# Copying a shifted matrix in 4 KB pieces down a column, 128 rows per DMA, in place of half rows of 16 KB, 1024 rows per DMA

## Chip, cores, metric

One core of a Trainium2 chip; the seven other cores are idle. The metric is the device time of one execution in microseconds. The kernel before takes 812.68 us (median of 3 runs, 810.87 to 816.9). On the chips of the experiments the same kernel takes 814 to 827 us, so every comparison in time is with runs of the kernel before on the same chip.

## The reference

```python
x = np.random.randn(8192, 8192).astype(np.float32)   # 268 MB

def reference(x):
    return np.fft.ifftshift(x)     # both halves swapped, in both directions
```

Every element moves by 4096 rows and 4096 columns, modulo 8192. No arithmetic is done. The longest run of bytes that stays together is half a row: 4096 x 4 bytes = 16 KB.

## The kernel before

Four quadrants, each copied from memory to memory by four DMAs, all issued from one queue:

```python
    quads = [
        ((0, hr), (0, hc), (hr, R), (hc, C)),
        # ... the other three quadrants in the same way (cut)
    ]
    nsplit = 4
    for (or0, or1), (oc0, oc1), (ir0, ir1), (ic0, ic1) in quads:
        step = (or1 - or0) // nsplit                 # 1024 rows
        for s in range(nsplit):
            a = s * step
            b = a + step
            nc.sync.dma_start(
                out=out[or0 + a : or0 + b, oc0:oc1],
                in_=x[ir0 + a : ir0 + b, ic0:ic1],
            )
```

Of the kernel before, what the change touches and what calls it, by code (L numbers as in the profile page):

```python
# [1 line left out]

# [4 lines left out]


@with_exitstack  # L10
def kernel(
    ctx: ExitStack,
    tc: tile.TileContext,
    x: bass.AP,
    out: bass.AP,
):
    nc = tc.nc

    R, C = x.shape
    hr = R // 2  # L20
    hc = C // 2

    quads = [
        ((0, hr), (0, hc), (hr, R), (hc, C)),
        ((0, hr), (hc, C), (hr, R), (0, hc)),
        ((hr, R), (0, hc), (0, hr), (hc, C)),
        ((hr, R), (hc, C), (0, hr), (0, hc)),
    ]

    engines = [nc.sync]  # L30
    nsplit = 4
    k = 0
    for (or0, or1), (oc0, oc1), (ir0, ir1), (ic0, ic1) in quads:
        rows = or1 - or0
        step = rows // nsplit
        for s in range(nsplit):
            a = s * step
            b = a + step
            eng = engines[k % len(engines)]
            k += 1  # L40
            eng.dma_start(
                out=out[or0 + a : or0 + b, oc0:oc1],
                in_=x[ir0 + a : ir0 + b, ic0:ic1],
            )


# [1 line left out]
_INS = ['x']  # L48
_OUTS = [((8192, 8192), 'float32')]


def kernel(**inputs):
    import numpy as _np
    import concourse.bacc as _bacc
    import concourse.tile as _tile
    from concourse import mybir as _mybir
    from concourse.bass_utils import run_bass_kernel_spmd as _run

    nc = _bacc.Bacc("TRN2", target_bir_lowering=False, num_devices=1)  # L59
    arrays, args = {}, []  # L60
    for name in _INS:
        a = _np.ascontiguousarray(inputs[name])
        if a.dtype.kind in "iu":
            a = a.astype(_np.int64)
        arrays[f"in_{name}_dram"] = a
        args.append(nc.dram_tensor(f"in_{name}_dram", a.shape, _mybir.dt.from_np(a.dtype), kind="ExternalInput").ap())
    for i, (shape, dtype) in enumerate(_OUTS):
        dt = _mybir.dt.from_np(_np.dtype(dtype))
        args.append(nc.dram_tensor(f"out_{i}_dram", shape, dt, kind="ExternalOutput").ap())
    with _tile.TileContext(nc) as tc:  # L70
        kernel(tc, *args)
    r = _run(nc, [arrays], core_ids=[0])
    got = tuple(r.results[0][f"out_{i}_dram"] for i in range(len(_OUTS)))
    return got[0]
```

## Time and profile before

| | before |
|---|---|
| median | 812.68 us |
| profiled span | 811.5 us |
| DMAs, each | 16, 16.8 MB |
| data packets, each | 16384, 16 KB |
| busy time of the 16 DMA engines | 99.3% |
| memory read + written | 662 GB/s |

The lines behind this table are in the prediction. The compute engines have nothing to do, so only the DMA part of the page speaks. "Busy" there means that an engine had a packet under way; whether the packet moved at full speed shows only in how long it took. A data packet here is one unbroken piece that one engine moves; a completion write is a packet of 4 bytes with which an engine reports that its share of a DMA is done. The time that a data packet takes beyond the commonest, shortest one of its size is called its stall.

### The profile page before, as it was taken

Reading aid. Unit: us, or ns where it says so; the run is one execution under the profiler, and the core shown is the slowest. Engines: PE = TensorE matmul, PEld = TensorE weight load, DVE = VectorE, ACT = ScalarE, POOL = GpSimd, SP = SyncE. Lnnn points to the kernel's source line nnn. Section 1 sums busy time; section 2 is a strip of 40 time slices with the busy share of each in tenths; the row PEclk is TensorE's granted clock in tenths of the full one; section 3 lists DMA queues with packets and bytes.
Section 4 is the critical chain, followed back from the end, with each engine's and each line's share of the span. In section 5 each row is a group of like instructions: output and inputs, shape, how many; then the busy total and the mean of one; then the engine's idle time right before and its main releaser. Section 6 shows DMA issues by size and latency. Waiting matters only on the chain. (4 is left out here: it accounts for less than half of the span.)

```text
span 811.5 us, 61 instructions
## 1 busy us (share of the span) xinstructions
POOL 0.2 (0%) x4
## 2 busy tenths in 40 slices
POOL 0000000000000000000000000000000000000000
DMA  9999999999999999999999999999999999999998
GB/s 298 328 328 333 312 337 332 326 334 329 332 334 329 329 329 334 331 331 334 338 340 333 332 334 339 334 333 337 338 333 337 334 333 338 332 334 341 328 339 287
DMA packets 16640, 268.44 MB, mean 331 GB/s; under 512 B 256, under 2 KB 256, under 8 KB 256
## 3 DMA queue, kind: packets, MB, share of 16 engines
q1 hardware_dynamic: 16640, 268.44, 99.3%
HBM read 268.44 MB, written 268.44 MB: 662 GB/s over the span
## 5 line engine op out<-in xcount | busy, mean ns | idle before, releaser
L59 POOL MEMSET const-bfloat16-1.0<- 128x1 bf16 x1 | 0.1, 102 | 0.0
L59 POOL MEMSET const-uint8-127<- 128x1 uint8 x1 | 0.1, 101 | 0.0
L59 POOL MEMSET const-float32-0.0<- 128x1 f32 x1 | 0.1, 99 | 0.2 <-issue 0.2
L59 POOL MEMSET const-float32-1.0<- 128x1 f32 x1 | 0.1, 98 | 0.0
## 6 DMA issues: line engine op xcount, KB each, us to landing
out_dram<-in_x_dram SPq DMA_DIRECT2D x16, 16384.0 KB, 158.0
```

Of the source, the lines that this page charges most:

```text
L59: nc = _bacc.Bacc("TRN2", target_bir_lowering=False, num_devices=1)
```

## The change

The intent is to give the memory a better order of addresses. Half rows are cut in four pieces of 4 KB; one DMA takes one column of pieces, 128 rows deep, so that an engine's next piece lies one row (32 KB) further on, and not right behind the last.

```diff
+ROWS_PER_DMA = 128
+PIECE = 1024
...
-    for (or0, or1), (oc0, oc1), (ir0, ir1), (ic0, ic1) in quads:
-        rows = or1 - or0
-        step = rows // nsplit
-        for s in range(nsplit):
             ... (cut)
-            eng.dma_start(
-                out=out[or0 + a : or0 + b, oc0:oc1],
-                in_=x[ir0 + a : ir0 + b, ic0:ic1],
+    for row in range(0, R, ROWS_PER_DMA):
+        src = (row + hr) % R
+        for col in range(0, C, PIECE):
+            oc = (col + hc) % C
+            nc.sync.dma_start(
+                out=out[row : row + ROWS_PER_DMA, col : col + PIECE],
+                in_=x[src : src + ROWS_PER_DMA, oc : oc + PIECE],
             )
```

More of the change, by code (lines that the diff above doesn't have):

```diff
@@ L21 @@
     hc = C // 2
-    quads = [
-        ((0, hr), (0, hc), (hr, R), (hc, C)),
-        ((0, hr), (hc, C), (hr, R), (0, hc)),
-        ((hr, R), (0, hc), (0, hr), (hc, C)),
-        ((hr, R), (hc, C), (0, hr), (0, hc)),
-    ]
-    engines = [nc.sync]
-    nsplit = 4
-    k = 0
-    for (or0, or1), (oc0, oc1), (ir0, ir1), (ic0, ic1) in quads:
-        rows = or1 - or0
-        step = rows // nsplit
-        for s in range(nsplit):
-            a = s * step
-            b = a + step
-            eng = engines[k % len(engines)]
-            k += 1
-            eng.dma_start(
-                out=out[or0 + a : or0 + b, oc0:oc1],
-                in_=x[ir0 + a : ir0 + b, ic0:ic1],
+    for row in range(0, R, ROWS_PER_DMA):
[5 more added lines that the diff above has]
+                in_=x[src : src + ROWS_PER_DMA, oc : oc + PIECE],
             )
```

## The prediction

> **What bounds the kernel now.** I read the page from the top, then its queue lines, then the issues, then the packets one by one. The kernel is pure copying, memory to memory, with no compute: part 1 has four memory fills on POOL, 0.2 us in all, and the chain of part 4 ends with them, so neither says anything about the end. The slices and the queue lines do:
>
> ```profile
> DMA  9999999999999999999999999999999999999998
> GB/s 298 328 328 333 312 337 332 326 334 329 332 334 329 329 329 334 331 331 334 338 340 333 332 334 339 334 333 337 338 333 337 334 333 338 332 334 341 328 339 287
> DMA packets 16640, 268.44 MB, mean 331 GB/s; under 512 B 256, under 2 KB 256, under 8 KB 256
> ...
> q1 hardware_dynamic: 16640, 268.44, 99.3%
> HBM read 268.44 MB, written 268.44 MB: 662 GB/s over the span
> ```
>
> All 16 DMA engines are occupied all the time (99.3%), at a level rate of 326 to 341 GB/s in most slices; there is no head or tail to win (the first slice has 298, the last 287). Of the 16640 packets, 256 are the completion writes (16 DMAs by 16 engines) and 16384 the data: 268.44 MB / 16384 = 16 KB, one half row each.
>
> Occupied is not the same as running at full speed. From the trace's packet records: the mean data packet lasts 787 ns, the median 731, and 1024 of them per engine make 1024 x 0.787 = 806 us of the 811.5. But the shortest last 608 ns, and 35% are within 7 ns of that; the tail reaches 2.05 us. 608 ns for 16 KB is 26.9 GB/s, an engine's own pace. Had all run so, an engine would need 1024 x 0.608 = 623 us. So 183 us of each engine's time is packets waiting on memory. That is the quantity the change can touch.
>
> The issue side is not the limit:
>
> ```profile
> L41 SPq DMA_DIRECT2D out_dram<-in_x_dram x16: 582/49353/95664, 0.7 to 652.6; - x16
> ...
> DMA to landing us min/median/max: 53.7/158.0/199.5
> ```
>
> An issue into an empty queue took 0.58 us; the median of 49 us is SP held back by a full queue (one 16.8 MB DMA takes 16.8 / 0.331 = 50.7 us). The last issue is in place long before the end. The completion records also show that the 16 engines finish each DMA within 1.0 to 2.7 us of each other, even after 800 us. They advance together, within about three of their packets.
>
> **What the Trainium skill says.** "HBM Reference", Specifications (TRN2), gives 716 GB/s for the memory that a pair of cores shares. The trace has 662 GB/s of reads and writes together, 92% of that, if x and out both lie in that one memory. I take this as the ceiling: 536.87 MB / 716 = 750 us, as an estimate from that page, plus the 5 us at the ends.
>
> "DMA: Bandwidth & Descriptors", Latency and other measured facts, row "HBM row pitch at large powers of two": copies of 128 rows of 16 KiB ran at 207 GB/s per direction with a pitch of 512 KiB, 164 at 2 MiB, 103 at 4 and 8 MiB; 4 KiB of padding restored the rate, 192 B did not. It calls the mechanism (streams in lock step that fall on the same memory channels) an inference. It bears directly on this case: engines here advance together. No view says which rows an engine gets. If each gets a consecutive run, which is how I read the change's own words, then engine e starts 64 rows x 32 KB = 2 MiB after engine e-1. The broad mixture of full-speed and stalled packets agrees with streams that collide now and then; it does not prove it.
>
> "DMA: Bandwidth & Descriptors", Why small descriptors are slow, gives about 3 cycles per packet as fixed overhead. At its 850 MHz that is 3.5 ns, times 3072 more packets per engine = 11 us on the 623 us of full-speed time (estimate). Of the same page, the section on its rules recommends at least 1 MiB per DMA; here the DMAs shrink to 0.5 MiB. The trace before shows only 16 MiB DMAs, so it neither agrees nor disagrees.
>
> **The change, part by part.**
>
> Bytes: unchanged, 268.44 MB each way.
>
> DMAs: 16 become 8192/128 x 8192/1024 = 64 x 8 = 512, each 128 rows x 4 KB = 524 KB, so 8 data packets per engine. At today's 331 GB/s one such DMA is 1.58 us of work. SP needs about 0.58 us to issue one (the shortest of the row above; I have no issue of the new shape), plus some tens of ns between issues: 512 x 0.65 = 333 us, beside the transfers. The issuer is thus needed about 40% of the time. The trace has eight completion semaphores in turn, so up to eight DMAs, 8 x 1.58 = 12.7 us of work, should be in flight; the first packet starts 1.4 us after the first issue, so the latency of a DMA (estimate 1.4 + 1.6 + 1 = 4 us) fits inside. Cost on the path: 0, with some risk.
>
> Completion writes: 16 x 16 = 256 become 8192. Each lasts 9 ns in the packet records, and the number of active engines doesn't dip around them (16.0 to 16.1 of 16 before and after). So 512 x 9 ns = 4.6 us per engine in place of 0.14: +4.5 us.
>
> Data packets: 1024 of 16 KB per engine become 4096 of 4 KB. At full pace that is about 152 ns each, plus the overhead: 623 + 11 = 634 us. That isn't the bound while memory allows at most 750, so 0 on the path; it eats some slack.
>
> Memory side, where the sum is decided: the distance between two engines working at the same time falls from 2 MiB to 8 rows x 32 KB = 256 KiB, below the pitch at which the skill still has the full rate. An engine's requests in flight[...] now lie in several rows and not in one or two long runs, so a busy place in memory holds up a smaller part of them. Against it, all engines work in one 4 KB column at a time, on reads and on writes; only the row bits of the address tell them apart. If 60% of the gap to the ceiling is recovered: the stream goes from 806 to 806 - 0.6 x (806 - 750) = 772 us. With +4.5 for completion writes and 5.5 for the ends as now: about 782 us, 3.8% faster.
>
> **The rivals.**
>
> 1. The shared memory is simply full. At 92% of the nominal rate with reads and writes mixed, there may be nothing to recover, whatever the order. For it: the level GB/s row, and engines that keep together as under fair sharing. Against it: 35% of the packets run at the engine's own pace, which is odd for a resource that is always full. Then the time is 806 + 4.5 + 5.5 = 816 us, the same.
>
> 2. 4 KB pieces are worse for memory. Four visits to a row in place of one long run, and the 32 KB stride keeps the low address bits equal over all 16 engines and over source and destination (they differ by 16 KB in column). If those bits choose the channel, collisions grow. For it: the skill's row shows that regular pitches can halve the rate. Against it: there the pitches up to 512 KiB were harmless. A 5 to 15% loss would make 850 to 930 us.
>
> 3. The small DMAs bind: SP's issue, or the waits for a semaphore to come round, take over. It would need over 1.58 us per issue, 2.7 times what the shortest one took. If it came to 1.7 us, 512 x 1.7 = 870 us. I hold this least likely.
>
> 4. The ceiling isn't one memory's 716 GB/s (x and out may lie apart), and the new order removes nearly all stalls. Then the engines bind: 634 + 4.5 + 5.5 = 644 us. Unlikely, as I'd expect both tensors in the core's own memory.
>
> **Range and chances.** I give the recovery (main case) 0.52, rival 1 a good 0.24, rivals 2 and 3 together 0.24. The recovery centres at 770 to 785, bounded by 760 or so where the ceiling is reached; rival 4 lies under the range, and the heavier half of rival 2 above it. That leaves 745 to 855 for eight in ten.
>
> **What would show it right or wrong.** Right: DMA share still 99% or so, GB/s at 340 to 350 in every slice, packets of 4 KB with a mean of 185 to 192 ns (787 / 4 = 197 now) and a larger share near 152 ns, completion writes still about 9 ns, SP's issues mostly held back by a full queue. Rival 1: a mean packet of 197 ns and 331 GB/s. Rival 2: DMA share of 99% with packets clearly over 200 ns. Rival 3: DMA share that drops to 90% or less, with gaps between packets and SP's issues back to back. The working is wrong in its basis if the full-pace packet isn't near 152 ns, or if an engine isn't given consecutive rows.

## The result, and the profile after

The changed kernel takes 824.36 us (median of 4 runs, 820.41 to 825.46) against 813.75 us for the kernel before in 4 runs. The ratio is 1.0114, 95% interval 1.0076 to 1.0152: clear of 1. (Ratios here are the mean time of one kernel's fast runs over that of the other's in the same rounds, so not quite the ratio of the medians.) So the change cost 1.1%, where 3.8% had been forecast as gain.

The slices, queue and issue lines of the changed kernel's page, and the line of its issues (ns each, shortest, median and longest) from the view of the tile:

```profile
DMA  9999999999999999999999999999999999999998
GB/s 298 325 330 328 330 329 329 330 333 331 329 327 331 326 326 333 328 329 331 327 330 331 329 330 328 327 331 329 331 330 328 337 326 333 331 333 328 331 335 289
DMA packets 73733, 268.50 MB, mean 328 GB/s; under 512 B 8193, under 2 KB 8193, under 8 KB 73729
...
q1 hardware_dynamic: 73728, 268.47, 99.3%
...
HBM read 268.44 MB, written 268.44 MB: 656 GB/s over the span
...
out_dram<-in_x_dram SPq DMA_DIRECT2D x512, 512.0 KB, 12.7
...
L33 SPq DMA_DIRECT2D out_dram<-in_x_dram x512: 511/511/737, 0.7 to 806.0; - x171
```

The 8193 packets under 512 B are the completion writes (512 DMAs by 16 engines) and one instruction fetch; the other 65536 are the pieces. Engines are busy for 99.3% of the span as before, and most slices, 31 of 40, are a little lower than before. The engines have no gap; the issuer is held back by its own completions, as its waits show (engine, line, what it waited for, us in total, times, longest):

```profile
SPq L33 <- DMA out_dram<-in_x_dram: 534.4, 503, 2.0
```

534 us of SP's 819 are waiting, and an issue takes 0.511 us in the median. It has eight DMAs out at a time (12.7 us from issue to landing, 8 x 1.59 = 12.7).

The difference between the two kernels is in the packet records of the two traces:

| packets of the profiled run | before | after |
|---|---|---|
| data packets per engine, bytes | 1024 of 16 KB | 4096 of 4 KB |
| commonest time of one (full pace) | 611 ns | 159 ns |
| share of packets within 7 ns of that time | 35% | 85% |
| mean | 786.8 ns | 197.3 ns |
| 99th percentile | 1412 ns | 769 ns |
| all data packets, per engine | 805.6 us | 808.2 us |
| completion writes, 9 ns each, per engine | 0.14 us | 4.62 us |

Two things look right and are traps. Of the packets 85% now run at full pace, which looks like the hoped-for order; but the rest are stalled the longer, and the mean of four pieces is 4 x 197.3 = 789 ns, against 787. At full pace alone an engine would now need 4096 x 159 ns = 651 us, where it needed 1024 x 611 ns = 626; its stalls came down from 180 us to 157, and the total stayed. The engines became slower by themselves, and waited less by nearly as much. And the sum seems to close perfectly: 2.6 us more for data and 4.5 us more for completion writes are the 7.1 us by which the span grew (811.5 to 818.6). Since the engines are never idle in either kernel, the packet times *must* add up to the span; the sum says nothing about what caused the growth. The experiments below show that the completion writes did not.

### The profile page after: what moved, and what is told of

It is laid out like the page before. It is cut to its first block, busy times and chain, and to the rows that moved or that the text cites. A ratio compares the mean times of both kernels' runs of the same rounds, so it can differ in the third digit from the quotient of the medians.

```text
span 818.6 us, 557 instructions
## 1 busy us (share of the span) xinstructions
POOL 0.2 (0%) x4
## 2 busy tenths in 40 slices
DMA packets 73733, 268.50 MB, mean 328 GB/s; under 512 B 8193, under 2 KB 8193, under 8 KB 73729
## 3 DMA queue, kind: packets, MB, share of 16 engines
q1 hardware_dynamic: 73728, 268.47, 99.3%
## 6 DMA issues: line engine op xcount, KB each, us to landing
out_dram<-in_x_dram SPq DMA_DIRECT2D x512, 512.0 KB, 12.7
```

## The experiments

Theory F, formed from the result: the 16 engines together are held by what the memory takes in reads and writes, some 660 GB/s, whatever the order. Rival C: collisions of address streams stall the packets, so that order and distance matter. Rival P: the size of the piece itself costs. Rival R: each packet meets a stall of its own, whatever else runs. (The diffs below are shortened: where they name ROWS_PER_DMA and PIECE, the kernels that ran have the numbers written out.)

### Piece and DMA size apart

**p4k_1024rows**, the pieces of the change with the DMA depth of before:

```diff
-ROWS_PER_DMA = 128
+ROWS_PER_DMA = 1024
```

> 4 KB pieces down a column as in the changed kernel, but 1024 rows per DMA as in the kernel before: 64 DMAs, 1024 completion writes. Theory F (the memory that x and out share is full with some 660 GB/s of reads and writes, whatever the order; the 1.1% lost by the change is the completion writes, 512 x 9 ns = 4.6 us per engine, and about 2.5 us from the pieces): 1.003 of the kernel before, the mean data packet 197 ns. Rival P (the pieces cost it all): 1.01. Rival C (what stalls the packets is where the addresses fall, and engines 2 MiB apart collide more than engines 256 KiB apart): mean data packet clearly off 197 ns, over 205, and 1.04 or more.

Measured: 841.62 us, ratio 1.0188 (1.0138 to 1.0237). Its completion writes take 0.62 us per engine, and still it loses, so the completion writes are not where the loss is. Its mean packet was 202.0 ns; the changed kernel itself, run again on a later chip (below), had 201.6. The mark that rival C had set, 205, was not reached; the ratio is above F's 1.003 and also above rival P's 1.01. Part of it is an uneven end: in the slices of its page (the GB/s row, 40 equal slices of 21 us) the last one has 209.

```profile
GB/s 291 325 325 322 322 321 327 325 321 322 320 324 321 319 330 319 322 321 315 328 321 327 329 317 329 322 324 324 319 328 323 310 333 326 323 326 319 330 322 209
```

**p16k_32rows**, the other way round: 16 KB pieces, as many DMAs and completion writes as in the changed kernel:

```diff
-ROWS_PER_DMA = 128
-PIECE = 1024
+ROWS_PER_DMA = 32
+PIECE = 4096
```

> 16 KB pieces as in the kernel before, but 32 rows per DMA: 512 DMAs of 0.5 MB, 8192 completion writes as in the changed kernel. Theory F: the completion writes alone, +4.5 us, so 1.005 to 1.006 of the kernel before, mean data packet still 787 ns. Rival P: 1.000. Rival C: engines now 64 KiB apart and not 2 MiB, so the mean data packet moves away from 787 ns by 3% or more.

Measured: 825.13 us, ratio 0.9986 (0.9939 to 1.0032), mean packet 794 ns. Its records hold 4.61 us of completion writes per engine, and the time has not grown. So the prediction's "+4.5 us" is not in the time (a ratio of 1.0054 lies outside the interval). That an engine which is stalled for a quarter of its time does its 9 ns writes at nobody's cost is a reading of this, not measured by itself. The 794 ns are to be taken beside 787 with care: the kernel before was profiled on the first chip alone, and takes 1.6% longer on this one. Nor did engines 64 KiB apart, in place of 2 MiB, gain anything.

### Fewer engines

Row counts that 16 does not divide leave some engines without work. The loop is the same in all of these; it copies 16 KB pieces:

```diff
+    for row in range(0, R, hr):
+        src = (row + hr) % R
+        for col in (0, hc):
+            oc = (col + hc) % C
+            a = 0
+            for n in COUNTS:    # k8: 4 x 1016, 4 x 8;  k12: 4 x 996, 108, 4
+                                # k13: 4 x 1014, 39, 1;  k14: 4 x 1022, 8
+                nc.sync.dma_start(
+                    out=out[row + a : row + a + n, col : col + hc],
+                    in_=x[src + a : src + a + n, oc : oc + hc],
+                )
+                a += n
```

**k8**

> 16 KB pieces, row counts of 1016 and 8 that let only 8 of the 16 DMA engines work. Theory F: 8 engines at their own pace ask the memory for 8 x 26.9 x 2 = 431 GB/s, far below 660, so the stalls vanish: mean data packet 608 to 620 ns, 2048 x 0.61 = 1250 us. Rival C (collisions of streams): the stalls fall about with the number of streams, mean packet 690 ns, 1420 us. Rival R (a stall that each packet meets by itself, as from latency or refresh): 787 ns, 1615 us.

**k12**

> The same with 12 of 16 engines (row counts 996, 108 and 4). Theory F: the 12 ask for 646 GB/s at their own pace, just below the limit, so the time is 1365 x 0.608 = 830 us plus a little queueing, 835 to 860 us, although a quarter of the engines is idle. Rival C: mean packet 735 ns or so, 1005 us. Rival R: 1075 us.

Measured: k8 takes 1249.55 us with a mean packet of 611.2 ns; k12 takes 839.48 us with 612.9 ns. Slices, packets and traffic of k12's page:

```profile
DMA  6777777777777777777777777777777777777776
GB/s 280 326 315 319 325 317 323 323 325 322 325 322 325 322 325 322 325 323 322 320 325 323 325 323 325 323 325 323 325 323 325 323 325 323 325 319 321 324 324 260
DMA packets 16640, 268.44 MB, mean 320 GB/s; under 512 B 256, under 2 KB 256, under 8 KB 256
...
q1 hardware_dynamic: 16640, 268.44, 74.9%
HBM read 268.44 MB, written 268.44 MB: 641 GB/s over the span
```

As theory F had said (1250 us, and 835 to 860), the stalls are gone in both. In k12 the engines are busy 75% of the time, that is, a quarter of them stands idle at any time, and the kernel is 1.5% slower than with all 16. This is the central result. Twelve engines meet practically no stall while they draw 641 GB/s; four more engines add 1.5% in speed and, in the kernel before, 787 - 608 = 179 ns of stall to each packet. Rival R (787 ns) is out, and so is C in the form that was put down (690 and 735 ns). One more thing changed beside the number of engines: with these row counts an engine's share is 127 or 83 rows, so that engines, if each gets consecutive rows, no longer lie a power of two apart, as they do in every run with all 16. The next two runs answer that.

**k13** and **k14** (shares of 78 and 73 rows) ask how the step from 12 to 16 runs, and whether fewer streams could do better than 16.

> 13 of 16 engines, 16 KB pieces (row counts 1014, 39, 1). Run with 12 engines hardly a packet stalled at 641 GB/s. Theory F1 (a fixed ceiling of 650 to 660 GB/s on this chip): 13 engines could do 1260 x 0.608 = 766 us by themselves, the memory holds them to about 820 us, ratio 0.99 to 1.00, mean packet 640 to 650 ns. Theory F2 (the ceiling is higher, and too many streams at once bring it down): 770 to 795 us, ratio 0.94 to 0.97, mean packet 612 to 630 ns.

> 14 of 16 engines (row counts 1022 and 8). F1: the time of 16 engines, ratio 0.99 to 1.00, mean packet 690 to 700 ns. F2: 750 to 800 us, ratio 0.92 to 0.97, mean packet 640 to 680 ns.

Measured: k13 846.73 us, ratio 1.0278 (1.025 to 1.0305); k14 870.0 us, ratio 1.0564 (1.0539 to 1.0589). Both expectations fell: more engines than 12 made it *slower*, until with 16 it is fast again. The mean packets of 16 KB, 648.9 and 690.4 ns, are just what F1 had said. While all their engines work, the packet records show what one more engine does (stretch from 5 to 45 us of each trace; k12 and p16k_32rows ran on one chip, k13 and k14 on another):

| engines | run | each way | mean packet |
|---|---|---|---|
| 12 | k12 | 324 GB/s | 611 ns |
| 13 | k13 | 322 GB/s | 659 ns |
| 14 | k14 | 326 GB/s | 704 ns |
| 16 | p16k_32rows | 326 GB/s | 800 ns |

The rate stays, and each packet takes longer in proportion to the number of engines. The stalls come back at distances of 78 and 73 rows, so it was not the odd distance that removed them in k12: it was the smaller demand.

The time of k13 and k14 goes elsewhere. Slices of k14:

```profile
DMA  7888888888887888858888887687888868878754
GB/s 289 328 331 326 329 331 323 325 325 334 326 319 306 328 332 324 327 244 313 323 319 322 325 325 296 272 320 299 323 323 319 331 252 328 326 310 324 276 217 176
```

The rate starts at the same 326 to 331 GB/s as with 16 engines, then has dips, and ends at 217 and 176. The completion records say why: of the first DMA's 14 engines, with 73 packets each, six finished 45.9 to 46.8 us after its first packet had started, and eight after 55.8 to 56.6 us; at full pace it would be 44.6. In k13, with 78 packets each (47.7 us at full pace), five finished after 48.9 to 49.3 us and eight after 53.5 to 54.0. So there are two groups of engines, 8 and the rest, and the limit seems to be shared out to groups, not engines: 331 GB/s in halves is 165 each; six engines want 6 x 26.9 = 161 and get 155, while eight want 215 and get 170, or 21 each. In k13 five want 135 and get 130, and the eight have 190. Since the rows are dealt out evenly, the larger group ends last, alone: the last slice but one of k14, with 217 GB/s, is at the 215 that eight engines reach by themselves in k8. This reading is from completion times and rates; the records don't name the engines.

### One direction at a time

**load_only** and **store_only** give wrong results on purpose:

```diff
+    pool = ctx.enter_context(tc.tile_pool(name="t", bufs=8))   # load_only
+    for row in range(0, R, 128):
+        for col in (0, hc):
+            t = pool.tile([128, hc], mybir.dt.float32)
+            nc.sync.dma_start(out=t, in_=x[row : row + 128, col : col + hc])
+    nc.sync.dma_start(out=out[0:128, 0:hc], in_=t)
```

In store_only one tile of zeros goes to all of `out` in the same loop.

> Wrong result on purpose: x is only loaded, in 128 DMAs of 128 rows of 16 KB, to eight on-chip buffers in turn; one tile is stored at the end. If it is the sum of reads and writes that is full, not the reading: all engines at their own pace, mean packet 608 to 620 ns, 630 to 645 us. If reading alone were the limit at 331 GB/s: 810 us.

> Wrong result on purpose: one on-chip tile of zeros stored 128 times over the whole of out. If the sum is full: mean packet 608 to 620 ns, 630 to 645 us. If writing alone were the limit at 331 GB/s: 810 us.

Measured: 639.36 and 638.1 us, mean packets 615 and 617 ns. A few lines of each page, load first:

```profile
DMA packets 18577, 270.55 MB, mean 424 GB/s; under 512 B 2064, under 2 KB 2064, under 8 KB 2064
...
HBM read 268.44 MB, written 2.10 MB: 424 GB/s over the span
```

```profile
DMA packets 18433, 268.45 MB, mean 422 GB/s; under 512 B 2048, under 2 KB 2048, under 8 KB 2048
...
HBM read 0.00 MB, written 268.44 MB: 422 GB/s over the span
```

Neither reading nor writing alone is held at 331 GB/s; all 16 engines run at their own pace when each byte touches the memory once.

### Order and distance of the pieces

Four kernels on one chip. **after_again** is the changed kernel unaltered.

> The changed kernel once more, unaltered, as the yardstick on this chip for the three beside it: 1.011 of the kernel before, as on record (1.008 to 1.015).

Measured: 834.64 us, ratio 1.013 (1.0112 to 1.0148), mean packet 201.6 ns.

**p4k_same_row** takes two pieces of each of 64 rows in one DMA:

```diff
+    for row in range(0, R, 64):
...
+            for b in (0, 1):
+                nc.sync.dma_start(
+                    out=out[row : row + 64, col : col + hc].rearrange("r (a b f) -> r b a f", a=2, b=2)[:, b],
+                    in_=x[src : src + 64, oc : oc + hc].rearrange("r (a b f) -> r b a f", a=2, b=2)[:, b],
+                )
```

> 4 KB pieces and 512 DMAs as in the changed kernel, but each DMA takes two pieces, 8 KB apart, of each of 64 rows, so every other step of an engine stays in its row. If the order of the pieces matters as the change intends (one row apart is better): slower than the changed kernel by 2% or more. If only the size of the piece matters (theory F, ceiling a little lower for 4 KB): 1.01, within 0.5% of the changed kernel.

Measured: 844.44 us, ratio 1.0248 (1.0215 to 1.0282), 1.2% slower than after_again. That lies between the two expectations. The slices of the two kernels, after_again first:

```profile
GB/s 290 322 320 328 322 327 319 325 326 325 323 325 319 327 324 325 329 322 328 319 326 326 324 329 326 325 328 320 325 324 327 320 324 327 321 321 326 326 320 276
```

```profile
GB/s 241 293 295 304 314 328 332 317 327 327 327 321 324 327 324 328 328 318 321 313 324 331 319 323 330 325 319 324 321 329 333 319 330 319 320 326 327 323 326 269
```

After the first five slices the rates are alike, around 324. The loss is in the start: 49 + 29 + 25 + 24 + 8 = 135 GB/s short over slices of 21 us, or 135 x 21 / 324 = 9 us, nearly the whole difference (844.44 - 834.64 = 9.8). So this other way of cutting is worse than going down the column, the change's idea, but in the one profile only in the first 100 us. Why this order starts slowly is not known.

**p2k_256rows** halves the piece and **p16k_4096rows** spreads the engines furthest:

```diff
-ROWS_PER_DMA = 128
-PIECE = 1024
+ROWS_PER_DMA = 256      # p16k_4096rows: 4096
+PIECE = 512             # p16k_4096rows: 4096
```

> 2 KB pieces down a column, 256 rows per DMA, so still 512 DMAs of 0.5 MB and 8192 completion writes; twice the packets. If the piece is what lowers the ceiling: 1.02 or more of the kernel before, more than the changed kernel. If not: as the changed kernel, 1.01. The engines alone would need 8192 x 83 ns = 680 us (152 ns / 2 plus the 7 ns that a packet costs at 4 KB), so they don't bind.

> 16 KB pieces, 4096 rows per DMA, so 4 DMAs, and engines that work 256 rows = 8 MiB apart (if an engine gets consecutive rows). Theory F: the mean data packet stays at 787 to 795 ns, ratio 1.00 to 1.01 (a longer uneven end). If the distance between engines matters[...]: mean packet over 900 ns, ratio 1.15 or more.

Measured: p2k_256rows 835.68 us, ratio 1.0142 (1.0124 to 1.016), like the changed kernel beside it and not more; p16k_4096rows 823.56 us, ratio 0.9998 (0.9981 to 1.0015), mean packet 796 ns. The distance between engines makes no difference here at 64 KiB (p16k_32rows), 2 MiB (the kernel before) and 8 MiB, if an engine gets consecutive rows, which no record shows. All three are powers of two; with all 16 engines no other distance was tried.

### What the limit counts, and where the piece begins to cost

**mix11** puts a second queue beside the copy, which loads all of x to buffers that nobody reads; **mix21** loads half of x, in 8 KB packets:

```diff
+            nc.sync.dma_start(
+                out=out[row : row + 128, col : col + hc],
+                in_=x[src : src + 128, oc : oc + hc],
+            )
+            t = pool.tile([128, 4096], mybir.dt.float32)       # mix21: 2048
+            nc.scalar.dma_start(out=t, in_=x[row : row + 128, col : col + 4096])   # mix21: 2048
```

> The whole copy in 16 KB pieces on one queue, and beside it, on a second queue, all of x loaded to on-chip buffers that nobody reads (correct result, superfluous loads), 16 KB packets each, so the engines should alternate. Sum theory: 537 MB through engines that can move 428 GB/s make 1.5 bytes of memory traffic per byte, 642 GB/s, just under the limit; hardly a stall, mean packet 612 to 640 ns, 1255 to 1310 us. If only copies are slow, (787 + 612)/2 = 700 ns, 1435 us.

> The same with half as many bytes of loads, in 8 KB packets, so two bytes copied per byte loaded: 403 MB through the engines, 671 MB of memory traffic. Sum theory: 671 / 0.66 = 1017 us, stalls again although writes run at only 265 GB/s. Writes-alone theory (limit 331 GB/s of writes): the engines bind, 403 / 0.428 = 941 us, no stalls.

Measured: mix11 1252.17 us, mean packet 611.7 ns, both just below what the sum theory had put down (1255 us, 612 ns). Traffic and queues of its page:

```profile
DMA packets 36866, 536.90 MB, mean 429 GB/s; under 512 B 4096, under 2 KB 4096, under 8 KB 4096
...
q10 hardware_dynamic: 18432, 268.44, 50.2%
q1 hardware_dynamic: 18432, 268.44, 50.1%
...
HBM read 536.87 MB, written 268.44 MB: 644 GB/s over the span
```

All 16 engines work at full pace, and in half of their packets they copy. So a copy packet is not slow in itself, nor does a 16-engine program stall of itself; at 644 GB/s of traffic there is no stall, as in k12.

mix21 takes 1067.94 us; 1017 and 941 had been expected, so it fits neither. The slices:

```profile
GB/s 372 399 405 408 417 409 416 399 418 421 397 413 418 415 410 412 419 410 410 402 407 418 397 414 396 340 335 333 334 334 320 339 332 332 336 333 334 330 338 230
```

The assumption of two bytes copied per byte loaded was wrong: while both queues ran, the records have 202 GB/s of copies and 209 of loads (100 to 500 us), and after the loads were done the copy went on alone at its usual 333. In the first part the traffic is 2 x 202 + 209 = 613 GB/s, *less* than mix11's 644, and yet packets stall a little: 629 ns for 16 KB and 325 ns for 8 KB in the mean, against 611 and 309 at full pace, 3 to 5% (in the part without loads it is 785 ns). So writes alone are not the limit, for these run at 202 GB/s there; but the sum of bytes is no fixed number either. It depends on what the streams look like; here, with loads of 8 KB in between, a little waiting sets in at 613. The packet records say one thing more, if each packet's bytes are spread evenly over its time. In mix21 loads and copies alternate unevenly: of the 200 steps of 2 us from 100 to 500 us, 75 carry over 700 GB/s, with packets 0.5% over full pace, while in the steps under 600 they are 6 to 13% over it. In mix11 81 of 550 steps carry over 700 GB/s without a stall. So the limit of some 650 GB/s holds for the mean over longer stretches; from moment to moment the stalls do not follow the sum.

**p8k_64rows**

```diff
-ROWS_PER_DMA = 128
-PIECE = 1024
+ROWS_PER_DMA = 64
+PIECE = 2048
```

> 8 KB pieces, 64 rows per DMA, 512 DMAs, 8192 completion writes. If the loss grows smoothly as pieces shrink: 1.005 to 1.008 of the kernel before. If it sets in below half a row: either 1.000 or 1.013.

Measured: 812.41 us, ratio 0.9983 (0.9958 to 1.0008). At 8 KB nothing is lost, at 4 KB 1.3%, at 2 KB 1.4%: the loss sets in below 8 KB and does not follow the number of packets. This kernel too goes down a column, has 512 DMAs and 8192 completion writes, so none of these is what costs by itself. How often the walk comes back to a row grows as the piece shrinks, and was not tested apart from it. What happens between 8 and 4 KB stays open.

No version was found that beats the kernel before: p8k_64rows, p16k_32rows and p16k_4096rows are all within 0.2% of it.

## Why the prediction was wrong

**What held.** The engines are busy all the time, at a level rate, and 183 us per engine are time beyond full pace. The issuer is off the path: it waits 534 us in the changed kernel, and an issue takes 0.51 us (0.58 had been assumed). The pace of a 4 KB packet is 159 ns (152 plus overhead had been said). The completion write takes 9 ns. Rival 3 did not occur, nor did rival 4.

**The step that failed** is the memory side: "If 60% of the gap to the ceiling is recovered: the stream goes from 806 to 806 - 0.6 x (806 - 750) = 772 us." Nothing was recovered: the data packets take 808.2 us per engine. The term of 34 us is 0, or rather -2.6, and for two reasons. First, the ceiling was set at 716 GB/s of nominal rate; in the runs a copy in 16 KB pieces gets 652 to 662 over the span with 16 engines, in each order and at each distance tried, and 641 with 12. The kernel before already stood at what is to be had. Secondly, the stalls were taken for collisions that another order would avoid. That 12, 13, 14 and 16 engines move the same 322 to 326 GB/s, at 611, 659, 704 and 800 ns a packet, shows that the stall is queueing: the surplus demand of 16 engines (431 GB/s each way at full pace against 331) has to wait somewhere, and none of the orders tried shortened that wait. The row of the Trainium skill on which the hope of 256 KiB in place of 2 MiB rested ("DMA: Bandwidth & Descriptors", Latency and other measured facts) speaks of the pitch between the rows of one copy. The prediction set the distance between engines in its place; the rows of a copy lie 32 KB apart before and after.

**The misreading behind it** is in the first rival: "35% of the packets run at the engine's own pace, which is odd for a resource that is always full." It is not odd. In the changed kernel 84% run at full pace, at the same total rate. How waiting is spread over packets depends on how the bytes are cut; the mean per byte is what carries information.

**Rival 1** was the right mechanism, and its sign, a mean packet of 197 ns, came true (197.3). Its time was 816 us against 812.68, a ratio of 1.004; measured was 1.0114. Its 4.5 us for completion writes are refuted (0.9986 and 0.9983 with just as many), and 1.3% for pieces of 4 KB, in none of the rivals at that size, comes in their place. **Rival 2** had the direction of this, but at 5 to 15%, and by equal low address bits; p8k_64rows has the column walk without a loss. (Its own sum, 5 to 15% more than 806 us and the ends, is 856 to 937 us, not 850 to 930.) That 824 us lies within the stated 745 to 855 us is no credit to the working: the range took in both gain and loss.

**What stays open.** Where the limit lies, in the memory or on the way to it, and what it counts: read plus written bytes fit the runs with pieces of 8 and 16 KB but for mix21, and only as a mean; the two groups of engines in k13 and k14 show only that it is shared out by groups. Whether x and out lie in one memory was assumed, not shown. The loss between 8 and 4 KB, the slow start of p4k_same_row, and the stalls at 613 GB/s in mix21 have no explanation here.

## What to carry to other kernels

When engines are always busy but their packets last longer than the shortest ones, take engines away before rearranging addresses: if fewer engines give nearly the same rate without stalls, as 12 of 16 do here, the stalls are a queue in front of a full resource, and another order of requests has little to win; none of those tried here shortened it. Don't read a cause into packet times that add up to the span, since with engines that are never idle they always do; and use row counts that load all 16 engines evenly, for 13 and 14 engines were slower than 12.

## What the Trainium skill lacked or had wrong

- "HBM Reference", Specifications (TRN2): 716 GB/s for the shared memory is not what one core's copy reaches; 652 to 662 GB/s of reads and writes together with 16 KB pieces, 641 with 12 engines, 613 in the mixed phase of mix21. The page has no rate for copies from memory to memory. The rate of a core that streams alone, about 425 GB/s, agrees: 424 loading, 422 storing.
- "DMA: Bandwidth & Descriptors", Latency and other measured facts, the row on the row pitch at large powers of two: nothing of the kind appears when only the distance between *engines* is large and each engine's rows are 32 KB apart (0.9998 at 8 MiB, 0.9986 at 64 KiB, if an engine gets consecutive rows). The row doesn't say that it is limited so; its accesses were different ones. The rate that it calls full for copies between HBM tensors, 214 GB/s per direction, is passed by far here (331 before); why its copies were slower is not known.
- The same page, Why small descriptors are slow: about 3 cycles per packet. The prediction made 3.5 ns of them with the 850 MHz that the page gives for the fabric, which is its own step. From the full-pace times here, 611, 309, 159 and 84 ns for 16, 8, 4 and 2 KB, the fixed part is about 8 ns and the rest 27.2 GB/s ((16384 - 4096) B / (611 - 159) ns). It was off the path.
- The same page, Rules for kernel authors: at least 1 MiB per DMA. DMAs of 0.5 MiB, eight in flight, cost nothing here in pieces of 8 or 16 KB (0.9983, 0.9986). The page doesn't name 4 KB pieces as a cost in copies; here they are 1.3%.
- The same page, Queues, rings and completion order: arbitration between queues is by packet, of several descriptors. In mix21 a queue of 8 KB pieces got as many bytes as one of 16 KB pieces (209 and 202 GB/s), so twice as many pieces; its turns were not one recorded piece each. How the bytes are shared between queues with pieces of different sizes, the page doesn't say.
- No page read here says that engines share the memory in groups: with 14 engines six finished their 73 packets after 46 us and eight after 56 us, and the copy took 1.056 of the time of 16 engines, where 12 took 1.015.
